# Four projections as half-size block products in a stage of their own, and a merge laid out by tokens

## The chip, the cores and the metric

The kernel runs on one core of one Trainium2 chip. The time is that of one execution on the device in microseconds (us), the median of three runs. TensorE (PE) multiplies matrices into PSUM, VectorE (DVE) and ScalarE (ACT) work on SBUF and PSUM, GpSimd (POOL) on SBUF alone; SyncE (SP), ScalarE and GpSimd have queues from which DMAs start.

## What is computed

One layer of a hybrid decoder for 512 tokens of width 1024, in float32. The parts of it that matter here:

```python
h = rms_norm(x, mixer_norm)
q, k, v, g_out, a_lr, z, xbc, dt, gate_a, gate_b = split_cols(h @ w_in)   # v, g_out, gate_a, gate_b: 1024 wide
o_a = gla_mixer(q, k, v, g_out, a_lr, ...)      # 4 heads, dk 128, dv 256, chunks of 64; o * rsqrt(mean(o*o)) * silu(g_out)
o_b = ssd_mixer(z, xbc, dt, ...)                # 2048 wide, 4 groups, chunks of 128
merged = sigmoid(gate_a) * (o_a @ w_branch_a) + sigmoid(gate_b) * (o_b @ w_branch_b)
x = x + merged @ w_out
h = rms_norm(x, ffn_norm)
act, lin = split(h @ w_ffn_up)                  # 2816 each
x = x + (gelu(conv3(act)) * lin) @ w_ffn_down
x = x + sigmoid(rms_norm(x, ple_norm) @ w_ple_gate) * (p @ w_ple_proj)
return rms_norm(x, final_norm)
```

## The kernel before

Every float32 product is made of three fast ones. An operand is split into a rounded part and the rest: `wsplit` (L160) lets ScalarE cast a raw weight tile to `whi` (L164) and VectorE subtract it to get `wlo` (L165), 1024 columns at a time. Three matmuls follow (`mm3`, L168, and the loops at L249 and L348): high by high, high by low, low by high. The normed activations lie turned, features on partitions, as `hT` (h1h and h1l, eight blocks of 128 features by 512 tokens). There are four buffers each of whi and wlo, and a ring of raw weight tiles, two up to the feed-forward part and five in it; raw tiles come by DMA from SP's queue (`wload`, L149).

`proj_a` holds weights still and moves activations, so that its result has features on partitions. `proj_b` holds activations still and moves 512 weight columns, so that its result has tokens on partitions. Both take PSUM banks from `mm_ps`, of which there are four; everything else (transposes, GLA's and SSD's small products) takes banks in turn from the other four, `sm_ps`.

The stages follow one another. SSD runs over four groups: x, B and C by `proj_a`, z by `proj_b`, the core of four chunks, the gate, and `ssd_branch` (L679), which multiplies a group's output by 512 rows of w_branch_b and adds it into `accb`, features on partitions. The last group's branch (L787) has a lower priority and so lies beside the start of GLA. GLA (L792 to L962) first makes the decay from a small gate product (`gg`, L807), then for each pair of heads the projections of v, of q and k, and of the output gate (`gla_pair_proj`, L828), and then one core per head (`gla_core`, L881). A core computes att and atc, masks them (L896), turns ks into kst, builds the state from u in four steps, makes the four outputs o, squares and sums them on ScalarE (L936), takes the root on GpSimd (`ors`, L357), gates them by `sg` on VectorE (L940) and turns them into `oah` and `oal`. Then come the merge gates (`gate_pair`, L970) by `proj_a`, with GpSimd multiplying the second gate by accb (L977), between pieces of w_branch_a (`branch_pair`, L985), which yield the merged activations turned already, `mth` and `mtl`. w_out by `proj_b`, the residual and the norm follow, then the feed-forward part.

The feed-forward down projection already uses seven half-size products in place of eight (`strassen`, L328, with `STEPS`, L279): activations are combined by `combine` (L289, VectorE), weight quarters are added by DMA (L318) or by GpSimd (L325), the products gather in three pairs of PSUM banks X, Y and Z, and after each step VectorE adds both banks into x.

A planner orders the instructions of each engine when the program is built. It simulates their times and takes what is ready by priority; `ahead` (L136) raises that of a weight's load and split and of the work that empties a bank. On the chip each engine and queue then goes through its list in order.

Of the kernel before, what the change touches and what calls it, by code (L numbers as in the profile page):

```python
# [43 lines left out]
def tile_hybrid_block(  # L44
# [128 lines left out]
    def proj_a(srcs, act, nk, emit, halves=False, raws=None):  # L173
# [26 lines left out]
        while i < len(srcs):  # L200
# [4 lines left out]
            for s in range(0, n, per):  # L205
                with ahead():
                    hi, lo = wsplit(raw[:, :, s * P : (s + per) * P], nk, per * P)
                for j in range(per):
                    ps = mm_ps(f"pa{uid()}")
                    for k in range(nk):  # L210
# [8 lines left out]
                        )  # L219
                    with ahead(50000):  # L220
                        emit(i + s + j, ps)
            i += n

    def proj_b(src, act, nk, emit, tail=False, split_last=False):
# [17 lines left out]
        for i, t in order:  # L242
# [46 lines left out]
    def combine(pool, g2, ch, cl, j):  # L289

        t = pool.tile([P, 4, 256], F32, tag="cmb", name=f"cmb{uid()}", bufs=1)
# [14 lines left out]

    def weights(r, v, parts, kh):


        n = len(parts)  # L310
        if n < 3:
            raw = r[parts] = rp[0].tile([P, kh, 512], F32, tag="raw", name=f"raw{uid()}", bufs=rp[1])
            for i, q in enumerate(parts):
                blk = v[int(q[0]) - 1][:, :, 512 * int(q[1]) - 512 : 512 * int(q[1])]
                if i == 0:
                    nc.sync.dma_start(raw, blk)
                else:
                    nc.gpsimd.dma_start(raw, blk, accum_op=ALU.add)  # L318
# [922 lines left out]
```

## Time and profile before

| | us |
|---|---|
| median of three runs | 1177.1 |
| lowest, highest | 1175.6, 1180.19 |
| the profiled execution | 1180.49 |
| its span, first to last instruction | 1178.5 |
| TensorE busy in the span | 1157.1 (98%) |
| VectorE | 677.4 (57%) |
| ScalarE | 520.5 (44%) |
| GpSimd | 171.1 (15%) |

The profile is one execution. A matmul's recorded duration overlaps those of its neighbours, so durations add up to more than the time they fill. In a group's row stand the line and engine, the operation, what it writes and reads, the count, the busy time and mean duration in nanoseconds, and the idle time ahead of it with what ended that.

### The profile page before, as it was taken

The numbers are of one execution on the slowest core, as the hardware profiler recorded it, in microseconds if no ns is written. First come the engines' busy times: TensorE is split into PE (matmuls) and PEld (weight loads), VectorE is DVE, ScalarE is ACT, GpSimd is POOL, SyncE is SP. The second block draws the span as 40 slices with busy tenths as digits, with TensorE's granted clock in tenths as the row PEclk, the third lists the DMA queues.
The fourth block names the chain that finished last, engine by engine and source line by source line (L and its number), as shares of the span: only waits on it lengthen the run. The fifth ranks groups of instructions, "written<-read, shape, count | busy, mean of one in ns | idle before, by whom it ended". The sixth has DMA issues, their size and how long they took to land.

```text
span 1178.5 us, 14049 instructions
## 1 busy us (share of the span) xinstructions
PE 1157.1 (98%) x5540; PEld 957.9 (81%) x5540; DVE 677.4 (57%) x864; ACT 520.5 (44%) x850; POOL 171.1 (15%) x175
## 2 busy tenths in 40 slices
PE   6999999999999999999999999999999999999997
PEld 6887887887887678888888888898888888888786
DVE  5767638667558537234234324565566755766764
ACT  4566373582383217442433222444434443344553
POOL 6103004022004000000011110100021000201313
PEclk9998999999999999999999999999999999999999
DMA  7332122222223134322224232752526453445221
GB/s 209 108 106 72 37 73 72 72 72 72 89 65 98 36 110 140 107 72 72 72 72 120 77 107 72 186 154 81 134 72 170 119 158 90 116 129 123 90 90 71
DMA packets 150177, 117.39 MB, mean 100 GB/s; under 512 B 5456, under 2 KB 124880, under 8 KB 150112
## 3 DMA queue, kind: packets, MB, share of 16 engines
q1 hardware_dynamic: 146624, 108.64, 31.6%
q0 software_dynamic: 2912, 5.77, 2.9%
q10 hardware_dynamic: 576, 2.10, 0.5%
q8 instruction: 43, 0.70, 0.3%
q14 instruction: 22, 0.18, 0.0%
HBM read 114.40 MB, written 2.10 MB: 99 GB/s over the span
## 4 chain that ended last, share of the span: by engine, by line
PE 96%; DVE 1%; DMA 1%; SPq 1%; POOL 1%; issue 0%; ACT 0%; POOLq 0%; ACTq 0%
PE pa L170 18%; PE pa L169 18%; PE pa L171 17%; PE pb L249 8%; PE pb L251 8%; PE pb L250 8%; PE yd L624 3%; PE sX L348 2%; PE sX L349 2%; PE sX L350 2%; PE st L632 1%; PE yo L621 1%; PE sZ L348 1%; PE sZ L349 1%; PE sZ L350 1%; DMA raw<-in_w_in_dram 1%
## 5 line engine op out<-in xcount | busy, mean ns | idle before, releaser
L165 DVE TENSOR_TENSOR wlo<-raw,whi 128x1024 fp32r<-128x1024 f32 (+1 forms) x208 | 261.5, 1263 | 255.2 <-ACT whi L164 255.0
L164 ACT CAST whi<-raw 128x1024 fp32r<-128x1024 f32 (+1 forms) x209 | 216.9, 1039 | 359.5 <-PE pa L170 219.2
L169 PE MATMUL pa<-h1h,whi 128*128 128x512 f32 (+1 forms) x416 | 160.5, 386 | 0.3 <-ACT h1h L419 0.3
L171 PE MATMUL pa<-h1h,wlo 128*128 128x512 f32 (+1 forms) x416 | 157.7, 379 | 0.0
L170 PE MATMUL pa<-h1l,whi 128*128 128x512 f32 (+1 forms) x416 | 157.0, 377 | 0.1
L169 PE MATMUL pa<-h2h,whi 128*128 128x512 f32 (+1 forms) x384 | 142.7, 372 | 0.0
L170 PE MATMUL pa<-h2l,whi 128*128 128x512 f32 (+1 forms) x384 | 142.6, 372 | 0.0
L171 PE MATMUL pa<-h2h,wlo 128*128 128x512 f32 (+1 forms) x384 | 142.3, 372 | 0.0
L249 PE MATMUL pb<-whi,h1h 128*128 128x512 f32 x256 | 99.7, 394 | 0.8 <-DVE accb L684 0.8
L250 PE MATMUL pb<-wlo,h1h 128*128 128x512 f32 x256 | 99.8, 390 | 0.0
L251 PE MATMUL pb<-whi,h1l 128*128 128x512 f32 x256 | 99.4, 392 | 0.0
L169 PEld LDWEIGHTS pa<-h1h,whi 128*128 128x128 f32 x416 | 79.9, 192 | 15.3 <-issue 1.2
L170 PEld LDWEIGHTS pa<-h1l,whi 128*128 128x128 f32 x416 | 79.6, 191 | 14.7 <-issue 1.0
L171 PEld LDWEIGHTS pa<-h1h,wlo 128*128 128x128 f32 x416 | 79.5, 191 | 13.8 <-issue 0.2
L171 PEld LDWEIGHTS pa<-h2h,wlo 128*128 128x128 f32 x384 | 72.3, 188 | 12.6
L169 PEld LDWEIGHTS pa<-h2h,whi 128*128 128x128 f32 x384 | 72.3, 188 | 12.5
L170 PEld LDWEIGHTS pa<-h2l,whi 128*128 128x128 f32 x384 | 72.3, 188 | 12.3
L249 PEld LDWEIGHTS pb<-whi,h1h 128*128 128x128 f32 x256 | 48.1, 188 | 10.6 <-DVE accb L684 1.2
L251 PEld LDWEIGHTS pb<-whi,h1l 128*128 128x128 f32 x256 | 48.1, 188 | 9.8
L250 PEld LDWEIGHTS pb<-wlo,h1h 128*128 128x128 f32 x256 | 48.1, 188 | 9.3
L549 DVE SCALAR_TENSOR_TENSOR acc<-pa,prm,acc 128x511 f32<-128x511 f32 (+2 forms) x72 | 52.6, 743 | 2.9 <-ACT acc L547 2.0
L170 PE MATMUL pa<-obl,whi 128*128 128x512 f32 x128 | 51.9, 406 | 0.0
(378 smaller groups left out, 1995.3 us busy)
## 6 DMA issues: line engine op xcount, KB each, us to landing
raw<-in_w_in_dram SPq DMA_DIRECT2D x48, 512.0 KB, 5.1
raw<-in_w_ffn_up_dram SPq DMA_DIRECT2D x44, 512.0 KB, 5.3
raw<-in_w_in_dram SPq DMA_DIRECT2D x16, 1024.0 KB, 5.1
raw<-in_w_ffn_down_dram SPq DMA_DIRECT2D x10, 1024.0 KB, 5.2
raw<-in_w_branch_b_dram SPq DMA_DIRECT2D x32, 256.0 KB, 4.1
raw<-in_w_branch_a_dram SPq DMA_DIRECT2D x8, 512.0 KB, 4.7
raw<-in_w_out_dram SPq DMA_DIRECT2D x4, 1024.0 KB, 5.1
raw<-in_w_ffn_down_dram POOLq DMA_DIRECT2D x4, 1024.0 KB, 8.6
```

The costliest lines, as they stand in the source:

```text
L164: S.copy(hi, raw)
L165: eng.tensor_tensor(lo, raw, f32(hi), op=ALU.subtract)
L169: TE.matmul(ps, lhsT=lh, rhs=rh, start=first, stop=False)
L170: TE.matmul(ps, lhsT=lh, rhs=rl, start=False, stop=False)
L171: TE.matmul(ps, lhsT=ll, rhs=rh, start=False, stop=last)
L249: TE.matmul(pss[t], lhsT=a, rhs=hi[:, kk, :], start=first, stop=False)
L250: TE.matmul(pss[t], lhsT=a, rhs=lo[:, kk, :], start=False, stop=False)
L251: TE.matmul(pss[t], lhsT=b, rhs=hi[:, kk, :], start=False, stop=last)
L348: TE.matmul(ps, lhsT=a_h, rhs=hi[:, k % 2, :], start=new and k == 0, stop=False, skip_group_check=True)
L349: TE.matmul(ps, lhsT=a_h, rhs=lo[:, k % 2, :], start=False, stop=False, skip_group_check=True)
L350: TE.matmul(ps, lhsT=a_l, rhs=hi[:, k % 2, :], start=False, stop=k == kh - 1, skip_group_check=True)
L549: V.scalar_tensor_tensor(out=acc[:, s:], in0=ps[:, : T - s], scalar=cw[:, ct, 3 - s : 4 - s], in1=acc[:, s:], op0=ALU.mult, op1=ALU.add,)
```

## The change

Four 1024-wide projections of h1 (v, the output gate, both merge gates) leave GLA and the merge and become a stage between SSD and GLA. Each is one `strassen` product of seven steps, in the order `ORDER`, with four raw quarters loaded once and summed on GpSimd in place (`weights_once`); its pieces are gathered in SBUF, put through their function and stored to DRAM from ScalarE's queue, 256 KB each. Blocks of h1 are used as they are; four further combinations of them are made once (`hc`), the sums by GpSimd. GLA's pairs and the merge load the pieces back from SP's queue. The ring has five raw tiles in the new stage, and two in GLA. w_branch_b, w_branch_a and accb are laid out by tokens (`proj_b`), so that the merged result is turned by TensorE (`transpose_split`) before w_out. In GLA ks, qi and the third exponential are made in place, kst and on have two buffers, sg six. The residual x2 reuses accb's buffers, and `ssd_gate` is parted from the turning of its result (`ssd_turn`). The core of the diff:

```diff
-    def combine(pool, g2, ch, cl, j):
...
+    ORDER = (0, 4, 1, 3, 2, 5, 6)
+    def combine(pool, g2, at, j, cs=(0, 3, 2, 5), eng=V):
         a1, a21, a22 = g2[:, :, :256], g2[:, 0, 256:], g2[:, 1, 256:]
-        V.tensor_tensor(t[:, 0, :], a22, a21, op=ALU.subtract)
-        V.tensor_tensor(t[:, 3, :], t[:, 0, :], a1[:, 0, :], op=ALU.add)
-        V.tensor_tensor(t[:, 1, :], a1[:, 0, :], a21, op=ALU.subtract)
-        V.tensor_tensor(t[:, 2, :], t[:, 3, :], a1[:, 1, :], op=ALU.subtract)
-        for c, src in ((slice(0, 2), a1), (2, a22), (3, t[:, 0, :]), (slice(5, 7), t[:, 1:3, :])):
-            S.copy(ch[:, c, j, :], src)
-            V.tensor_tensor(cl[:, c, j, :], src, f32(ch[:, c, j, :]), op=ALU.subtract)
-        S.activation(ch[:, 4, j, :], t[:, 3, :], AF.Copy, scale=-1.0)
-        V.scalar_tensor_tensor(
-            out=cl[:, 4, j, :], in0=t[:, 3, :], scalar=-1.0, in1=f32(ch[:, 4, j, :]),
-            op0=ALU.mult, op1=ALU.subtract,
-        )
+        def tmp():
+            return pool.tile([P, 2, 256], F32, tag="cmb", name=f"cmb{uid()}", bufs=2)
+        def put(c, n, src):
+            h, l, c = at(c)
+            c = slice(c, c + 2) if n == 2 else c
+            S.copy(h[:, c, j, :], src)
+            V.tensor_tensor(l[:, c, j, :], src, f32(h[:, c, j, :]), op=ALU.subtract)
+        if 0 in cs:
+            put(0, 2, a1)
+        if 3 in cs:
+            t = tmp()
+            eng.tensor_tensor(t[:, 0, :], a22, a21, op=ALU.subtract)
+            eng.tensor_tensor(t[:, 1, :], t[:, 0, :], a1[:, 0, :], op=ALU.add)
+            put(3, 1, t[:, 0, :])
+            h, l, c = at(4)
+            S.activation(h[:, c, j, :], t[:, 1, :], AF.Copy, scale=-1.0)
+            V.scalar_tensor_tensor(
+                out=l[:, c, j, :], in0=t[:, 1, :], scalar=-1.0, in1=f32(h[:, c, j, :]),
+                op0=ALU.mult, op1=ALU.subtract,
+            )
+        if 2 in cs:
+            put(2, 1, a22)
+        if 5 in cs:
+            t = tmp()
+            eng.tensor_tensor(t[:, 0, :], a1[:, 0, :], a21, op=ALU.subtract)
+            eng.tensor_tensor(t[:, 1, :], a22, a1[:, 1, :], op=ALU.subtract)
+            eng.tensor_tensor(t[:, 1, :], t[:, 1, :], t[:, 0, :], op=ALU.add)
+            put(5, 2, t)
...
-    def strassen(src, ch, cl, kh, add):
+    def weights_once(r, v, n, kh):
+        if not r:
+            for q in ("11", "12", "21", "22"):
+                r[q] = new_raw(kh)
+                nc.sync.dma_start(r[q], quarter(v, q))
+        dst, src = {0: ("11", 0), 4: ("21", 0), 1: ("11", "12"), 3: ("22", 0), 2: ("11", "22"), 5: ("12", "22"), 6: ("11", "21")}[n]
+        if src:
+            pool_sum(r[dst], r[src], kh)
+        return r[dst]
+    def strassen(src, get, kh, add, once=True, ybank=None):
         v = src.rearrange("(k two p) n -> two p k n", two=2, p=P)
         banks, r = {}, {}
-        for n, (c, parts, b, th, h, sign) in enumerate(STEPS):
+        for n in ORDER if once else range(7):
+            c, parts, b, th, h, sign = STEPS[n]
             with ahead():
-                raw = r[parts] if parts in r else weights(r, v, parts, kh)
+                raw = weights_once(r, v, n, kh) if once else weights(r, v, parts, kh)
                 ws = [wsplit(raw[:, k : min(k + 2, kh), :], min(2, kh - k), 512) for k in range(0, kh, 2)]
             new = b not in banks
             if new:
-                banks[b] = [sm_ps(f"s{b}{uid()}") for _ in range(2)]
+                banks[b] = [(ybank or sm_ps if b == "Y" else sm_ps)(f"s{b}{uid()}") for _ in range(2)]
...
+                    a_h, a_l = get(c, k, tok)
...
+    def project_out(off, fn, dst):
+        cnt, pcs = Parts(), {}
+        def add(t, h, ps, sign, n):
+            first, last = cnt(t, h)
+            if first:
+                pcs[t, h] = hsp.tile([P, T], F32, tag="pj", name=f"pj{uid()}", bufs=8)
+            pc = pcs[t, h]
+            if first and last:
+                S.activation(pc, ps, fn)
+            elif first:
+                S.activation(pc, ps, AF.Copy, scale=float(sign))
+            else:
+                V.tensor_tensor(pc, pc, ps, op=ALU.add if sign > 0 else ALU.subtract)
+                S.activation(pc, pc, fn)
+            if last:
+                nc.scalar.dma_start(dst[t][h], pc)
+        return strassen(w_in[:, off : off + 1024], hget, 4, add, ybank=mm_ps)
...
     def ssd_branch(g):
-        def emit(n, ps):
+        def emit(t, h, ps):
             if g == 0:
-                S.copy(accb[:, n, :], ps)
+                accb[t][h] = piece_of(f"accb{t}_{h}")
+                S.copy(accb[t][h], ps)
             else:
-                V.tensor_tensor(accb[:, n, :], accb[:, n, :], ps, op=ALU.add)
-        proj_a(
-            [w_branch_b[512 * g : 512 * (g + 1), n * P : (n + 1) * P] for n in range(KD)],
-            st[g]["ob"], 4, emit,
-        )
+                V.tensor_tensor(accb[t][h], accb[t][h], ps, op=ALU.add)
+        for h in range(2):
+            yield from proj_b_steps(
+                w_branch_b[512 * g : 512 * (g + 1), 512 * h : 512 * h + 512], st[g]["ob"], 4,
+                lambda t, ps, h=h: emit(t, h, ps), tail=True,
+            )
...
-    base = tc.cur_priority
-    tc.cur_priority = base + 1200
-    ssd_branch(SG - 1)
-    tc.cur_priority = base
+    run(ssd_branch(SG - 1))
     sx.close()
+    ex_ = ExitStack()
+    hsp = ex_.enter_context(tc.tile_pool(name="hsp", bufs=1, reuse_waits="tile"))
+    ring(ex_, 5)
+    hc = [hsp.tile([P, 4, 4, 256], R, name=f"hc{c}") for c in "hl"]
+    def h_at(c):
+        return hc[0], hc[1], c - 3
+    def hget(c, k, tok):
+        if c > 2:
+            return combs(h_at)(c, k, tok)
+        f = 2 * k + (c > 0)
+        tok = slice(tok.start + 256 * (c == 2), tok.stop + 256 * (c == 2))
+        return hT[0][:, f, tok], hT[1][:, f, tok]
+    dv = project_out(OFF_V, AF.Copy, vd)
+    run(dv, 2)
+    for j in range(4):
+        pr = hsp.tile([P, 2, T], F32, tag="pair", name=f"hpair{j}", bufs=1)
+        G.tensor_tensor(pr, f32(hT[0][:, 2 * j : 2 * j + 2, :]), f32(hT[1][:, 2 * j : 2 * j + 2, :]), op=ALU.add)
+        combine(hsp, pr, h_at, j, (3, 5), G)
+    run(dv)
+    run(project_out(OFF_G, AF.Silu, sgd))
+    run(project_out(OFF_GA, AF.Sigmoid, gad))
+    run(project_out(OFF_GB, AF.Sigmoid, gbd))
+    ex_.close()
...
-            E3 = gp.tile([P, T], F32, tag="E3", name=f"E3_{h}", bufs=2)
+            E3 = bc
...
-        v = v0 if hp2 == 0 else gp.tile([P, NT, 512], F32, tag="v", name=f"v{hp2}", bufs=2)
-        sg = gp.tile([P, NT, 512], F32, tag="sg", name=f"sg{hp2}", bufs=1)
-        proj_b(
-            w_in[:, OFF_V + 512 * hp2 : OFF_V + 512 * (hp2 + 1)], hT, KD,
-            lambda t, ps: S.copy(v[:, t, :], ps),
-        )
+        v = gp.tile([P, NT, T], F32, tag="v", name=f"v{hp2}", bufs=2)
+        sg = [gp.tile([P, T], F32, tag="sg", name=f"sg{hp2}_{t}", bufs=6) for t in range(NT)]
+        for t in range(NT):
+            nc.sync.dma_start(v[:, t, :], vd[t][hp2])
+        for t in range(NT):
+            nc.sync.dma_start(sg[t], sgd[t][hp2])
...
-        proj_b(
-            w_in[:, OFF_G + 512 * hp2 : OFF_G + 512 * (hp2 + 1)], hT, KD,
-            lambda t, ps: S.activation(sg[:, t, :], ps, AF.Silu),
         )
...
-        qi = gp.tile([P, T], F32, tag="qi", name=f"qi{h}", bufs=1)
-        S.copy(ev(qi, 0), ev(qtl, 0))
+        ks, qi = kpr, qtl
+        V.tensor_tensor(ev(ks, 0), ev(kpr, 0), dv[:, :, 1:2].to_broadcast([P, 4, 64]), op=ALU.mult)
         V.tensor_tensor(ev(qi, 1), ev(qtl, 1), dv[:, :, 0:1].to_broadcast([P, 4, 64]), op=ALU.mult)
-        ks = gp.tile([P, T], F32, tag="ks", name=f"ks{h}", bufs=1)
-        S.copy(ev(ks, 1), ev(kpr, 1))
-        V.tensor_tensor(ev(ks, 0), ev(kpr, 0), dv[:, :, 1:2].to_broadcast([P, 4, 64]), op=ALU.mult)
...
+    rp[:] = mring
+    gtp = gx.enter_context(tc.tile_pool(name="gtp", bufs=1, reuse_waits="tile"))
+    def gate(d, t, h):
+        gt = gtp.tile([P, T], F32, tag="gt", name=f"gt{uid()}", bufs=8)
+        nc.sync.dma_start(gt, d[t][h])
+        return gt
+    gas = [[gate(gad, t, h) for t in range(NT)] for h in range(1)]
+    for h in range(2):
+        for t in range(NT):
+            G.tensor_tensor(accb[t][h], accb[t][h], gate(gbd, t, h), op=ALU.mult)
     mtp = gx.enter_context(tc.tile_pool(name="mtp", bufs=1, reuse_waits="tile"))
...
-    gate_pair(0)
-    gate_pair(2)
-    branch_pair(0)
...
+    mt = tuple(mtp.tile([P, KD, T], R, name=f"mt{c}") for c in "hl")
+    def branch_a(h):
+        ga = gas[0] if h == 0 else [gate(gad, t, 1) for t in range(NT)]
+        def emit(t, ps):
+            ac = accb[t][h]
+            V.tensor_tensor(ga[t], ga[t], ps, op=ALU.mult)
+            V.tensor_tensor(ac, ac, ga[t], op=ALU.add)
+            transpose_split(ac, mt, t, h, f"mT{t}")
+        proj_b(w_branch_a[:, 512 * h : 512 * h + 512], (oah, oal), KD, emit, tail=h == 1)
+    for h in range(2):
+        branch_a(h)
+    x2 = [[piece_of(f"x2_{t}_{h}") for h in range(2)] for t in range(NT)]
+    for h in range(2):
+        for t in range(NT):
+            nc.sync.dma_start(x2[t][h], x[t * P : (t + 1) * P, 512 * h : 512 * h + 512])
...
```

## Rows read from the trace of the kernel before

**Rows 1.** The page: busy time by engine; the chain that ended last.

```profile
PE 1157.1 (98%) x5540; PEld 957.9 (81%) x5540; DVE 677.4 (57%) x864; ACT 520.5 (44%) x850; POOL 171.1 (15%) x175
...
PE 96%; DVE 1%; DMA 1%; SPq 1%; POOL 1%; issue 0%; ACT 0%; POOLq 0%; ACTq 0%
```

**Rows 2.** Waits, TensorE: waiter, awaited, us in all, times, longest.

```profile
PE xn0T L417 <- DVE xn L394: 7.4, 1, 7.4
...
PE pb L249 <- DVE accb L684: 0.8, 1, 0.8
...
PE sX L349 <- DVE wlo L165: 0.6, 1, 0.6
...
PE ot L670 <- DVE Xg L664: 0.2, 1, 0.2
```

**Rows 3.** Windows by stage: length, then busy (count) by engine, clock, DMA.

```profile
396.00:484.00 88.00, 87.22 (x371) 68.62 (x370) 43.77 (x60) 33.19 (x43) 0.00 (x0) 1.00 0.36 115
484.00:546.00 62.00, 62.00 (x300) 51.18 (x299) 25.10 (x40) 29.00 (x55) 3.73 (x8) 1.00 0.26 75
```

**Rows 4.** Timeline of TensorE, 121 to 128 us: start, duration.

```profile
121.24 0.40 PE L170 MATMUL pa<-h1l,whi 128*128 128x512 f32 x1
...
127.82 0.39 PE L169 MATMUL pa<-h1h,whi 128*128 128x512 f32 x1
```

**Rows 5.** Chain in order of time: start, length, what, matmul instructions.

```profile
509.98 0.43 PE o L921 x2
...
510.84 0.44 PE oaT L947 x4
511.28 0.89 PE att L890 x8
...
754.81 0.87 PE x2n0T L417 x8
```

**Rows 6.** Groups by line and form: GpSimd, VectorE, ScalarE.

```profile
L325 POOL TENSOR_TENSOR raw<-raw,raw 128x1024 f32<-128x1024 f32 x10 | 24.7, 2469 | 106.7 <-DVE wlo L165 106.7
...
L977 POOL TENSOR_TENSOR sgt<-sgt,accb 128x512 f32<-128x512 f32 x8 | 14.1, 1768 | 76.6 <-ACT sgt L975 76.6
...
L896 DVE TENSOR_TENSOR attT<-att,gmask 128x512 f32<-128x512 f32 x4 | 2.8, 692 | 1.8 <-PE att L890 1.8
...
L911 ACT COPY kstok<-kst 128x512 f32<-128x512 f32 x4 | 2.3, 579 | 1.6 <-PE kst L909 1.6
```

**Rows 7.** Timelines of VectorE, then of GpSimd, 870 to 890 us.

```profile
877.32 0.69 DVE L1087 TENSOR_TENSOR x<-x,sX 128x512 f32<-128x512 f32 x1
...
879.82 1.23 DVE L165 TENSOR_TENSOR wlo<-raw,whi 128x1024 fp32r<-128x1024 f32 x1
...
881.55 3.04 DVE L165 TENSOR_TENSOR wlo<-raw,whi 128x1024 fp32r<-128x1024 f32 x1
...
876.96 2.52 POOL L325 TENSOR_TENSOR raw<-raw,raw 128x1024 f32<-128x1024 f32 x1 [3.05 <-DVE wlo L165]
881.12 2.40 POOL L325 TENSOR_TENSOR raw<-raw,raw 128x1024 f32<-128x1024 f32 x1 [1.65 <-DVE wlo L165]
```

**Rows 8.** DMA issues: size of one, us from issue to landing.

```profile
raw<-in_w_in_dram SPq DMA_DIRECT2D x16, 1024.0 KB, 5.1
```

**Rows 9.** Timeline of the first GLA core, 509.5 to 519.5 us.

```profile
510.25 0.59 PE L923 MATMUL o<-gS,qi 128*128 128x256 f32 x2
...
511.16 0.19 ACT L936 ACTIVATION_READ_ACCUMULATOR on<-o 128x1 f32 x1
...
511.44 0.19 POOL L356 TENSOR_SCALAR ors<-oss 128x2 f32<-128x2 f32 x1 [5.56 <-ACT on L936]
...
512.82 0.87 DVE L940 SCALAR_TENSOR_TENSOR on<-o,ors,sg 128x256 f32<-128x256 f32 x2
```

**Rows 10.** Timeline of TensorE at 109 us, and a later window.

```profile
109.25 2.12 PE L624 MATMUL yd<-xdt,L 128*128 128x64 f32 x16 [1.58 <-DVE xdt L617]
...
118.00:120.00 2.00, 2.00 (x8) 1.48 (x8) 0.66 (x2) 0.76 (x3) 0.00 (x0) 0.50 0.05 12
```

More of the change, by code (lines that the diff above doesn't have):

```diff
@@ new lines, in combs, with get, quarter, new_raw @@
+    def combs(at):
+        def get(c, k, tok):
+            h, l, c = at(c)
+            return h[:, c, k, tok], l[:, c, k, tok]
+        return get
+    def quarter(v, q):
+        return v[int(q[0]) - 1][:, :, 512 * int(q[1]) - 512 : 512 * int(q[1])]
+    def new_raw(kh):
+        return rp[0].tile([P, kh, 512], F32, tag="raw", name=f"raw{uid()}", bufs=rp[1])
+    def pool_sum(dst, src, kh):
+        for k in range(0, kh, 2):
+            q = slice(k, min(k + 2, kh))
+            G.tensor_tensor(dst[:, q, :], dst[:, q, :], src[:, q, :], op=ALU.add)
@@ L317, in weights @@
                 else:
-                    nc.gpsimd.dma_start(raw, blk, accum_op=ALU.add)
+                    nc.gpsimd.dma_start(raw, quarter(v, q), accum_op=ALU.add)
             return raw
         raw, more = (r["11", "12"], "22") if n == 3 else (r["11", "12"], "21")
-        if (more,) not in r:
-            weights(r, v, (more,), kh)
-        for k in range(0, kh, 2):
-            q = slice(k, min(k + 2, kh))
-            G.tensor_tensor(raw[:, q, :], raw[:, q, :], r[more,][:, q, :], op=ALU.add)
@@ L326, in weights @@
-        return raw
-    def strassen(src, ch, cl, kh, add):
+        pool_sum(raw, weights(r, v, (more,), kh), kh)
+        return raw
+    def weights_once(r, v, n, kh):
[7 more added lines that the diff above has]
+        return r[dst]
@@ L353, in strassen, with __init__, __call__, ready @@
             yield
+    class Parts:
+        def __init__(self):
+            self.left = {}
+        def __call__(self, t, h):
+            total = 1 if (t // 2, h) == (1, 0) else 2
+            n = self.left.get((t, h), total)
+            self.left[t, h] = n - 1
+            return n == total, n == 1
+    class TileNorms:
+        def __init__(self, pool, tag, bufs, x, gain, dst, name):
+            self.a = pool, tag, bufs, x, gain, dst, name
+            self.nm = {}
+        def ready(self, t, h):
+            pool, tag, bufs, x, gain, dst, name = self.a
+            first = t not in self.nm
+            if first:
+                self.nm[t] = Norm(pool, x[t], f"{name}{t}", tag, bufs)
+            self.nm[t].square(h)
+            if first:
+                self.nm[t].gather()
+            else:
+                norm_T(self.nm[t], gain, dst, t)
+    def run(d, n=1000):
+        for _ in range(n):
+            if next(d, d) is d:
+                return
     def rsqrt_mean(dst, ssq, inv, n):
@@ L781, in tile_hybrid_block @@
         ssd_gate(g)
+        ssd_turn(g)
         if g + 1 < SG:
@@ L815, in tile_hybrid_block @@
         gtmp.append(e)
+    dx.close()
+    oap = gx.enter_context(tc.tile_pool(name="oap", bufs=1, side="right", reuse_waits="tile"))
+    oah = oap.tile([P, KD, T], R, name="oah")
+    oal = oap.tile([P, KD, T], R, name="oal")
+    glaring = rp[:]
+    ring(gx, 2, "right")
+    mring = rp[:]
+    rp[:] = glaring
     for h in range(GH):
@@ L985, in branch_pair @@
-    def branch_pair(n0):
-        def emit(i, ps):
-            n = n0 + i
-            s = gates[0, n]
-            V.tensor_tensor(s, s, ps, op=ALU.mult)
-            V.tensor_tensor(s, s, gates[1, n], op=ALU.add)
-            S.copy(mth[:, n, :], s)
-            V.tensor_tensor(mtl[:, n, :], s, f32(mth[:, n, :]), op=ALU.subtract)
-        proj_a([w_branch_a[:, (n0 + i) * P : (n0 + i + 1) * P] for i in range(2)], (oah, oal), KD, emit)
-    gate_pair(0)
-    gate_pair(2)
-    branch_pair(0)
-    gate_pair(4)
```

191 lines of the change are left out of this document (84 added, 107 removed).

## The prediction

> **What bounds the kernel now.** I read the page first: TensorE is busy for 98% of the span, VectorE for 57%, ScalarE for 44%, GpSimd for 15%, and the chain that ended last is TensorE for 96% [rows 1]. A busy TensorE may still be waiting inside a pipelined matmul, so the second view was what TensorE waited for: under 14 us in all, 9 of them in the start, and in the part that is changed a single wait of 0.8 us (ten rows, 13.7 us together) [rows 2]. The third was the windows by stage: from 396 to 546 us, which hold branch_b's last group, GLA's first projections and its first two cores, TensorE is busy 87.2 of 88 us and then 62 of 62, at full granted clock [rows 3]. So until about 775 us time is what TensorE issues. Removed matmuls count at their issue spacing, not at the mean that the groups print: in a stretch without gaps 29 matmuls of 512 columns start between 121.24 and 127.82 us, 0.2269 us each [rows 4].
>
> **The change part by part.** The sum is made against the profiled execution, 1180.5 us (span 1178.5). The median of the three runs, 1177.1, lies 3.4 lower, and I take that off at the end.
>
> *Matmuls removed.* The projections of values, output gates and the two merge gates are each 512x1024 times 1024x1024: 8 k blocks, 8 output tiles, 3 products, so 192 matmuls. As seven half-size products each takes 7 x 2 x 4 x 3 = 168. Four of them save 96, at 0.2269 us 21.8 us.
>
> *Transposes added.* Merge by tokens needs its result turned: 4 token tiles x 2 halves x 4 = 32 transposes. Eight take 0.87 us [rows 5], so 32 take 3.5. branch_b and branch_a keep their matmul counts (96 per group, 192) when the operands swap sides, and branch_b's adds into accb stay 512 wide. The ends are the same: +3.5.
>
> *Half-size products: who must keep up.* A step is 24 matmuls, 5.44 us, a projection 38.1. ScalarE has 14 casts, six copies and eight functions, which at 1.23 us each (a wlo of the same width as a cast, the widest of them) would be 34.4, so it keeps up. VectorE has 14 wlo subtractions, 1.23 us when alone [rows 7], and 6 adds from PSUM at 0.69: 17.2 + 4.1. GpSimd has four block sums of two 2.47 us pieces [rows 6]: 19.8. These are not independent. At 881.55 us a wlo that began while GpSimd summed took 3.04 us against 1.23, and it ended at 884.59, as one of some 1.1 us would that began when the sum ended at 883.52; an add from PSUM at 877.32, inside a sum that ran from 876.96, took 0.69 [rows 7]. So sums and wlo exclude each other: 17.2 + 19.8 = 37.0 of 38.1 us if the PSUM adds go beside the sums, and 41.1 if none do. That is a cost of 0 to 3.0 us a projection, 0 to 12 in all. [...] I take 2: adds arrive two to a step, there is room for them beside sums, and the first projection starts with a lead, as below. The combinations of the activations (GpSimd: four pairs of one 1024-wide and five 256-wide operations, 4 x (2.47 + 5 x 0.62) = 22.3 us, a quarter of the 1024-wide one taken for the narrow) are first needed at the third step. They read h1 alone, so the planner can put them under the last branch_b (96 matmuls, 21.8 us) and the first two steps (10.9): 32.7 us for 22.3 of work. Nothing is added; without that cover it would be 22.3.
>
> *DMA.* Weight blocks come as 1 MB, 5.1 us from issue to landing [rows 8], 20 of 38.1 us for four. The one late block reuses the buffer that the last sum of the projection before frees: some 2.4 us of splits, 5.3 to land, 4.9 of sums and 2.4 of splits make 15.0 us, from that buffer's last split, which can be done a step and a quarter before its products start, to the third step of the next projection, 17 us ahead at least. Hidden, by 2 us. The 32 stores of 256 KB sit on ScalarE's queue behind the function that made the piece, and the values are read a hundred us later. Behind them on ScalarE stand the next casts, a step ahead of need. The loads stand on SP's queue among weight loads; v and sg have the 21.8 us of the q and k projection to arrive.
>
> *From the last product to GLA.* The q and k weights go to memory that the combinations hold until the sixth of the seven steps ends. Then 5.1 us to land, and a cast and a wlo at 1.23 each: 7.6 us, against a last step of 5.44. Ends 0 (GLA's four small gate matmuls, whose weights have long been loaded, fill the rest) and 7.6; I take 2, the difference.
>
> *GLA's cores lose cover.* Before, the second pair's values, q, k and gates (65 us of matmuls) stood beside the first two cores and 87 us of merge gates beside the last two. Afterwards q and k alone (96 matmuls, 21.8 us) stand beside the first, and beside the last only branch_a's first half for heads 0 to 2: 72 matmuls, 16.3 us, 5.4 of it only when head 2 is done. The chain of one core, from rows: att and atc at most 0.89 each, mask 0.69 and ks 0.35 (half as wide; it is now in place, so after atc), kst 0.44 (four transposes, as oaT's four), its copy 0.58, u 0.43 (as o), its copy 0.29 (half as wide), then from the issue of the second o to the end of the gating 3.44 (510.25 to 513.69), u again 0.43 (its bank is one that the gating frees), the state 0.44 (as one gating), o to gating once more 3.44, oaT 2 x 0.44 [rows 5, 6, 9]: 13.2, and with 0.1 us at eight further hand-overs (an estimate from 511.35, where a sum was read out, to 511.44, where ors began) 14.0. The next core's att reuses a bank that the last gating frees, so a pair takes 28.0, of which 14.8 is TensorE's own (1.78 + 0.44 + ten of 0.43 + 0.88 a core). 13.2 us are waiting per pair. The first pair has 21.8 of cover. The second has 10.9 that is free from the start: 2.3 short, then some 1.4 for head 3's oah and oal (two as wide as the mask) before the last quarter of branch_a, and about 1 because ors stands on GpSimd behind accb's gating of 1.77 us an operation [rows 6]. Ends 0 and 13.2; I take 5.
>
> *At nothing:* the 0.8 us wait that goes with accb, the two copies per core that go, one more narrow operation per combine in the feed-forward part (its TensorE is full), x2 into accb's buffers (loaded 20 us ahead of use).
>
> Sum: -21.8 + 3.5 + 2 + 2 + 5 = -9.3. 1180.5 becomes 1171.2, and on the scale of the median **1168**.
>
> **The rivals.**
>
> *A, as summed:* 1168, give or take 5.
>
> *B, everything hidden.* -18.3: 1159. For it speaks the planner, which leaves no wait over 1.6 us after the start [rows 2, 10]; against it the cover that is used up beside the last two cores.
>
> *C, sums and wlo.* At the dear end the four projections take 12 us more than TensorE needs, not 2: 1168 + 10 = 1178, no change that can be measured (under 0.5%, 5.9 us). For it, the exclusion of [rows 7]; against it, that the down products of the feed-forward part show two such sums in a row and TensorE waits 0.6 us there in all [rows 2], though they have fewer sums per product (two of the seven blocks, where the change sums four).
>
> [...]
>
> That the change doesn't remove what it says can be left out: counts are in the code.
>
> **How the numbers follow.** A 0.45, B 0.18, C 0.22, D 0.15. Faster by over 0.5% is under 1171.2: A's part below it 0.37, B 0.18, a corner of C 0.04: 0.59. Same: A's upper edge 0.08 and C's middle 0.15: 0.23. Slower is above 1183: D and C's upper edge, 0.18. The range goes from B with a little to spare, 1156, to between C and D, 1185, leaving out most of D; the likeliest case's own is 1163 to 1173.
>
> **What would show it.** TensorE should issue 64 fewer instructions (96 less, 32 more). The stage of products should last 152.4 us with TensorE waiting for wlo for under 4; over 10 there is C. [...] It is wrong altogether if the part before 390 us or after the first feed-forward projection changes length by more than some us, since neither is argued here.

## Result, and the profile after

The changed kernel takes 1207.4 us (median of 4 runs, 1205.8 to 1211.4) against 1176.4 for the kernel before, run beside it: a ratio of 1.0245, 95% interval 1.0213 to 1.0277. It is 2.5% slower where 0.8% faster was forecast, and outside the range. Its profiled span is 1205.4 us, 26.9 longer.

The page of the changed kernel, as in [rows 1]: busy time by engine, and the chain that ended last.

```profile
PE 1152.9 (96%) x5476; PEld 947.7 (79%) x5476; DVE 780.1 (65%) x935; ACT 558.4 (46%) x899; POOL 293.4 (24%) x231
...
PE 85%; DVE 5%; POOL 3%; ACT 2%; issue 2%; DMA 1%; SPq 1%; ACTq 0%; POOLq 0%; DVEq 0%
```

TensorE issues the 64 instructions less that were counted, but it is busy only 4.2 us less, and idle 52.5 us of its span instead of 21.4. Where the idle time lies is seen in the windows of the changed kernel (length, then busy time and count by engine, granted clock, DMA share, GB/s), as in [rows 3]:

```profile
0.00:385.00 385.00, 371.65 (x1907) 307.71 (x1907) 255.11 (x306) 203.38 (x371) 86.98 (x88) 1.00 0.28 85
385.00:450.00 65.00, 55.22 (x230) 42.69 (x229) 54.43 (x47) 24.31 (x36) 53.98 (x33) 0.92 0.30 105
450.00:585.00 135.00, 133.46 (x579) 107.76 (x578) 98.93 (x71) 75.97 (x96) 75.31 (x27) 1.00 0.43 148
585.00:650.00 65.00, 57.27 (x247) 45.28 (x246) 33.97 (x49) 30.47 (x45) 0.91 (x2) 0.92 0.47 147
650.00:750.00 100.00, 92.92 (x445) 73.91 (x444) 50.90 (x83) 32.69 (x66) 17.03 (x22) 0.97 0.39 137
750.00:800.00 50.00, 45.07 (x236) 38.88 (x235) 23.01 (x30) 15.63 (x30) 4.05 (x12) 0.93 0.39 103
```

The kernel before is idle 11.8 us in the first of these stretches, 1.5 in the second and 0 in the others up to 800 us. So the 31 us are: 1.5 in the first, 8.3 about the first projection of the new stage, 1.5 in the rest of the stage, 7.7 at the step to GLA, 7.1 about the cores and 4.9 at the start of the feed-forward part.

The clock takes more. In the changed kernel TensorE's granted clock was 0.50 in six stretches between 394 and 795 us, each in or behind a hole in its work; in the kernel before in one, at 111 us [rows 10]. These are the windows at 0.50, the six as their sum, then the one before:

```profile
sum 34.00, PE 23.60 PEld 18.75 DVE 26.04 ACT 15.21 POOL 13.60; mean PE 3.93 PEld 3.13 DVE 4.34 ACT 2.54 POOL 2.27
110.90:121.20 10.30, 9.62 (x26) 5.97 (x26) 8.39 (x13) 5.18 (x8) 4.69 (x5) 0.50 0.37 104
```

In these stretches matmuls of 512 columns start 0.427 us apart (599.54 to 602.53 us in the changed kernel, at 0.50), against 0.227 from 603.22 us on, at 1.00. Here and below I count half of the busy time at 0.50 as lost, an estimate a little above what these two spacings give, 0.47: 11.8 of 23.6 us, against 4.8 of 9.6 before, 7.0 more. By the counts busy time should fall by 18.3 us, and it fell by 4.2. So 7.1 us are left that neither the counts nor the clock explain; they were not taken apart. Part of them may be that the last matmul ahead of a stop counts with its full 0.39 us, and not with the 0.23 to the next one.

What ended the idle time, TensorE's waits in the changed kernel, as in [rows 2] (waiter, awaited, us in all, times, longest):

```profile
PE pa L180 <- DVE wlo L174: 7.8, 2, 7.3
...
PE sX L418 <- ACT whi L173: 7.2, 2, 6.5
PE x2n3T L523 <- DVE x2n L500: 2.8, 1, 2.8
PE atc L1061 <- DVE attT L1066: 2.2, 2, 1.4
PE pa L178 <- ACT whi L173: 2.1, 3, 1.6
PE ot L813 <- DVE Xg L804: 2.0, 2, 1.7
```

Before, the longest wait in the changed part was 0.8 us. Now six pairs behind the start have 2 us or more in all.

**The first projection.** GpSimd's timeline in the changed kernel, in its third step and ahead of it (start, length):

```profile
390.03 2.36 POOL L954 TENSOR_TENSOR hpair<-h1h,h1l 128x1024 f32<-128x1024 f32 x1
...
422.93 2.85 POOL L366 TENSOR_TENSOR raw<-raw,raw 128x1024 f32<-128x1024 f32 x1
...
427.42 1.77 POOL L343 TENSOR_TENSOR cmb<-hpair 128x256 f32<-128x256 f32 x1
...
437.72 3.33 POOL L366 TENSOR_TENSOR raw<-raw,raw 128x1024 f32<-128x1024 f32 x1
441.01 1.71 POOL L330 TENSOR_TENSOR cmb<-hpair 128x256 f32<-128x256 f32 x1
```

Sums (`raw`) and combinations (`hpair`, `cmb`) alternate in one queue, and each is longer than priced: a 256-wide addition up to 1.77 us (priced 0.62), a sum up to 3.4 (2.47). The third step breaks off: TensorE stands still from 435 to 441.65 us, starts two matmuls of the fifth step, and goes on with the third at 443.21, with the combination whose `cmb` began at 441.01, behind the sum of 437.72. The two matmuls had waited for a cast on ScalarE that stood behind a piece of the step before; VectorE's addition to that piece stood behind a `wlo` of 2.78 us. From 443 to 446 the granted clock is 0.50; from 446 it is 1.00 again. The groups by line of the changed kernel (busy time, mean ns of one):

```profile
L174 DVE TENSOR_TENSOR wlo<-raw,whi 128x1024 fp32r<-128x1024 f32 x224 | 319.9, 1441 | 204.8 <-ACT whi L173 204.5
L366 POOL TENSOR_TENSOR raw<-raw,raw 128x1024 f32<-128x1024 f32 x42 | 119.9, 2866 | 163.3 <-DVE wlo L174 163.3
```

**The step to GLA.** VectorE and TensorE after the last product in the changed kernel (in brackets, idle time before and what ended it):

```profile
594.46 0.75 DVE L977 TENSOR_SCALAR ge<-gg,prm 128x512 f32<-128x512 f32 x1 [4.78 <-DMA v<-vd]
...
597.67 1.22 DVE L174 TENSOR_TENSOR wlo<-raw,whi 128x1024 fp32r<-128x1024 f32 x1
...
598.95 0.80 PE L180 MATMUL pa<-h1h,wlo 128*128 128x512 f32 x1 [7.29 <-DVE wlo L174]
```

The last gate tile `ge` lies in memory where a piece of the last product waits for its store; `wlo`, which TensorE needs, stands behind it on VectorE. The view names a load as the releaser, but `ge` waits for the semaphore that the store sent off at 588.50 raises (a load that waits for the same one left at 594.35), while the DMA engines were full (share 1.00, 327 GB/s, at 590 to 598 us).

**The feed-forward start.** SP's waits from 735 to 800 us in the changed kernel:

```profile
SPq L163 <- PE pb L271: 35.8, 1, 35.8
```

The second weight load lies over the merged activations, so it and all behind it in SP's queue wait for the output projection's last matmul. From the transposes of the third token tile to the end it is 424.4 us, 415.9 before: 8.5 lost after the part that the prediction argued. All of it lies at the start: from the 193rd matmul of the feed-forward part to the end it is 391.3 us, 391.2 before.

### The profile page after: what moved, and what is told of

It reads as the page before. It is cut to its first block, busy times and chain, and to the rows that moved or that the text cites. A ratio compares the mean times of both kernels' runs of the same rounds, so it can differ in the third digit from the quotient of the medians.

```text
span 1205.4 us, 14211 instructions
## 1 busy us (share of the span) xinstructions
PE 1152.9 (96%) x5476; PEld 947.7 (79%) x5476; DVE 780.1 (65%) x935; ACT 558.4 (46%) x899; POOL 293.4 (24%) x231
## 4 chain that ended last, share of the span: by engine, by line
PE 85%; DVE 5%; POOL 3%; ACT 2%; issue 2%; DMA 1%; SPq 1%; ACTq 0%; POOLq 0%; DVEq 0%
PE pa L180 11%; PE pa L178 11%; PE pa L179 11%; PE pb L269 8%; PE pb L270 8%; PE pb L271 8%; PE sX L418 4%; PE sX L419 3%; PE sX L420 3%; PE yd L763 2%; DVE wlo L174 2%; PE sZ L418 2%; PE sZ L419 2%; PE sZ L420 1%; POOL raw L366 1%
## 5 line engine op out<-in xcount | busy, mean ns | idle before, releaser
L174 DVE TENSOR_TENSOR wlo<-raw,whi 128x1024 fp32r<-128x1024 f32 (+1 forms) x232 | 325.9, 1419 | 210.8 <-ACT whi L173 210.5
L173 ACT CAST whi<-raw 128x1024 fp32r<-128x1024 f32 (+1 forms) x233 | 240.7, 1040 | 265.3 <-PE pa L179 141.7
L366 POOL TENSOR_TENSOR raw<-raw,raw 128x1024 f32<-128x1024 f32 (+1 forms) x44 | 123.4, 2817 | 167.3 <-DVE wlo L174 167.3
L180 PE MATMUL pa<-h1h,wlo 128*128 128x512 f32 (+1 forms) x288 | 108.3, 376 | 7.3 <-DVE wlo L174 7.3
L178 PE MATMUL pa<-h1h,whi 128*128 128x512 f32 (+1 forms) x288 | 109.3, 379 | 0.7 <-ACT whi L173 0.4
L179 PE MATMUL pa<-h1l,whi 128*128 128x512 f32 (+1 forms) x288 | 108.6, 377 | 0.1
L180 PEld LDWEIGHTS pa<-h2h,wlo 128*128 128x128 f32 x384 | 73.4, 191 | 13.2 <-DVE wlo L174 0.8
L178 PEld LDWEIGHTS pa<-h1h,whi 128*128 128x128 f32 x288 | 56.2, 195 | 11.6 <-ACT whi L173 1.7
L270 PE MATMUL pb<-wlo,obh 128*128 128x512 f32 x128 | 53.0, 414 | 0.0
L269 PE MATMUL pb<-whi,obh 128*128 128x512 f32 x128 | 52.4, 410 | 0.1
L271 PE MATMUL pb<-whi,obl 128*128 128x512 f32 x128 | 50.2, 396 | 0.0
L269 PE MATMUL pb<-whi,h1h 128*128 128x512 f32 x128 | 50.1, 394 | 0.0
```

Of the source, the lines that this page charges most:

```text
L173: S.copy(hi, raw)
L174: eng.tensor_tensor(lo, raw, f32(hi), op=ALU.subtract)
L178: TE.matmul(ps, lhsT=lh, rhs=rh, start=first, stop=False)
L179: TE.matmul(ps, lhsT=lh, rhs=rl, start=False, stop=False)
L180: TE.matmul(ps, lhsT=ll, rhs=rh, start=False, stop=last)
L269: TE.matmul(pss[t], lhsT=a, rhs=hi[:, kk, :], start=first, stop=False)
```

## Experiments

Each kernel is the changed one with the edit shown. Times are compared by the ratio to the kernel before that ran beside them.

| run | us | ratio to before | 95% interval | span |
|---|---|---|---|---|
| changed | 1207.4 | 1.0245 | 1.0213 to 1.0277 | 1205.4 |
| e1_vsum | 1197.7 | 1.0171 | 1.0126 to 1.0216 | 1202.9 |
| e2_vcomb | 1196.8 | 1.0164 | 1.0125 to 1.0203 | 1200.8 |
| e3_ringfirst | 1203.1 | 1.0208 | 1.0170 to 1.0246 | 1198.9 |
| e4_ffnring | 1207.8 | 1.0241 | 1.0204 to 1.0277 | 1205.0 |
| e5_gates | 1204.1 | 1.0225 | 1.0201 to 1.0249 | 1202.3 |
| e6_ffnearly | 1197.5 | 1.0181 | 1.0158 to 1.0205 | 1195.9 |
| e7_vboth | 1189.6 | 1.0115 | 1.0085 to 1.0145 | 1193.4 |
| e8_all | 1184.8 | 1.0062 | 1.0038 to 1.0086 | 1183.3 |
| e9_qkearly | 1173.1 | 0.9942 | 0.9920 to 0.9963 | 1171.7 |
| e10_gpsimd | 1184.4 | 1.0052 | 1.0029 to 1.0076 | 1182.6 |
| e11_gatev | 1172.9 | 0.9951 | 0.9928 to 0.9974 | 1171.4 |

**e1_vsum, e2_vcomb, e7_vboth: which engine adds.**

```diff
# e1
-            pool_sum(r[dst], r[src], kh)
+            pool_sum(r[dst], r[src], kh, V)
# e2
-        G.tensor_tensor(pr, f32(hT[0]...
+        V.tensor_tensor(pr, f32(hT[0]...
-        combine(hsp, pr, h_at, j, (3, 5), G)
+        combine(hsp, pr, h_at, j, (3, 5), V)
# e7: both
```

> The changed kernel with one edit: the block sums of the new stage's weights (12 of its 28 products, two adds of 1024 columns each) are made by VectorE instead of GpSimd; the combinations of the activations stay on GpSimd. Theory 1: GpSimd's sums and VectorE's low parts hold each other up (a sum 2.8 us on average instead of 2.5, a low part up to 3.7 instead of 1.23), and this starves the products. Then the sums cost VectorE about 1.2 us each with no exclusion, TensorE's idle time between 396 and 588 us falls by 8 to 12 us, and the kernel takes about 1197 (1193 to 1201). Rival: only the first projection is starved, by the combinations in GpSimd's queue, and the sums are harmless elsewhere. Then only what GpSimd's queue gains in the first projection shows, 2 to 4 us: 1203 to 1206.

> The changed kernel with one edit: the four additions of hidden high and low parts and the 20 sums of the combinations are made by VectorE instead of GpSimd; the block sums of the weights stay on GpSimd. Theory 1: the combinations cost what they cost because they stand on GpSimd, with the sums of the first projection behind them in its queue, and because they block VectorE's work of SSD's tail at 390 us. Then the hole of 5.8 us at 436 to 443 us goes, and the kernel takes about 1200 (1197 to 1203). Rival: VectorE has no room for them either, and the hole only moves to the low parts behind them: 1205 to 1209.

> The changed kernel with both the block sums of the weights and the combinations on VectorE (e1 and e2 together). Theory 1: what e1 and e2 gave (about 8.5 and 9 us by their ratios) came from different places, e1 from the three projections after the first, e2 from the first and the SSD tail, and adds up in part: about 1193 (1190 to 1197). Rival: VectorE is full in the first projection (35 to 39 of 39 us in e1 and e2), so both together starve TensorE there, and the kernel is no faster than either alone: 1196 to 1202.

`wlo` from 450 to 585 us in the changed kernel, then `wlo` and the sums there in e1:

```profile
L174 DVE TENSOR_TENSOR wlo<-raw,whi 128x1024 fp32r<-128x1024 f32 x47 | 84.9, 1839 | 26.2 <-ACT whi L173 26.0
...
L174 DVE TENSOR_TENSOR wlo<-raw,whi 128x1024 fp32r<-128x1024 f32 x47 | 57.3, 1222 | 25.4 <-ACT whi L173 24.8
L366 DVE TENSOR_TENSOR raw<-raw,raw 128x1024 f32<-128x1024 f32 x26 | 30.6, 1220 | 0.2
```

On VectorE a sum takes 1.22 us, and `wlo` is back at 1222 ns on average. From 450 to 585 us TensorE is then idle 0 us (1.5 in the changed kernel), so what engines can still win in the stage lies ahead of that: from 385 to 450 it is busy 55.2 us in the changed kernel, 57.8 in e1, 60.0 in e2, 62.2 in e7, out of 65. The gains of e1 and e2 there, 2.6 and 4.7, add up to about what e7 has, 7.0. By the ratios the gains are larger, 0.7%, 0.8% and 1.3%, some 9, 10 and 15 us. e1's profiled span is only 2.5 us shorter, but its profile has TensorE busy 13.0 us at a clock of 0.50 at 112 to 126 us, ahead of all that the edit touches, where the changed kernel's has none: 6.5 us lost, counted as above, that hide most of its gain. Theory 1 of e1 asked for 8 to 12 us less idle time by 588 us; it was 4.1. e7 shows that VectorE, busy 39 of 39 us at 397 to 436, does not become the bound by it: TensorE is busy for 38.6 of these 39.

**e3_ringfirst, e5_gates: the tiles at the step to GLA.**

```diff
# e3: the weight buffers of the stage first
+    ring(ex_, 5)
     hsp = ex_.enter_context(tc.tile_pool(name="hsp", ...))
-    ring(ex_, 5)
# e5: pieces in a pool of their own behind the combinations;
# GLA's gsm, ge, E1, E2 and on in a pool egp, which lies over hsp alone
+    pjp = ex_.enter_context(tc.tile_pool(name="pjp", ...))
-            pcs[t, h] = hsp.tile(
+            pcs[t, h] = pjp.tile(
+    egp = ggx.enter_context(tc.tile_pool(name="egp", ...))
```

> The changed kernel with one edit: the five weight buffers of the new stage are opened before its other tiles, so that the first gate tiles of GLA lie over a weight buffer and no longer over the pieces whose stores are the last to leave. Theory 1: the 7.3 us in which TensorE waits at 590 to 600 us for a low part come from the gate tile's wait for a store, with the low part queued behind it on VectorE. Then the stretch 585 to 600 us is nearly full, and the kernel takes about 1199 (1196 to 1202). Rival: the weights of Q and K are late anyway, since the DMA engines are full (328 GB/s) at 580 to 600 us; then the wait only changes its name: 1204 to 1208.

> The changed kernel with the pieces in a pool of their own behind the combinations, and GLA's gate and exponential tiles in a pool that lies over the combinations alone. Opening the weight buffers first (run e3) gave the 585 to 600 us stretch back, and then lost 8.8 us at the first attention product, because the gate chain still began at 589 us: its tiles lay over a pool that the list order could hand out only when all work on it had been placed. Theory 1: the tiles' place sets when the gate chain starts. It now starts about 15 us earlier, ahead of the low parts of Q and K, both waits go, and the kernel takes about 1193 (1189 to 1198), 13 less than the changed kernel by its ratio. Rival: GLA's start has too much serial work between the last product and the first attention product whatever the layout; then at most what e3 gave comes back: 1199 to 1204.

In e3 TensorE is busy all of 585 to 600 us (7.3 of 15 in the changed kernel), so the tiles' place over the stored pieces was the cause; but then its longest wait is a new one:

```profile
PE att L1060 <- DVE E L1022: 8.8, 1, 8.8
```

In e5 the gate chain starts at 582 us, 5 ahead of the last product's end (in e3 at 589, 2 behind it), both of these waits are gone, and the next one steps up:

```profile
PE pa L178 <- ACT whi L173: 7.5, 3, 4.2
```

5.8 us of this, in two waits, are for the high part of Q's first weights, whose buffer lies over the combinations until the last product that reads them. e3 gains 0.4% and e5 0.2%; their intervals overlap the changed kernel's. Theory 1 of e5 failed; the time is the one that its rival gave, but not by the rival's cause, as e9 shows below: with other places for the tiles the stretch from 585 to 600 us is full but for 0.7 us. Three waits stood one behind the other, and one edit alone only brought up the next.

**e4_ffnring, e6_ffnearly: the feed-forward start.**

```diff
# e4: the norm's tiles and 16 KB of nothing between the gates and mt
+    xnp = gx.enter_context(tc.tile_pool(name="xnp", ...))
+    pad = gx.enter_context(tc.tile_pool(name="pad", bufs=1)).tile([P, 4096], F32, ...)
     mtp = gx.enter_context(tc.tile_pool(name="mtp", ...))
# e6: the first two weight blocks in free memory, issued ahead of w_out's loop
+    f0p = gx.enter_context(tc.tile_pool(name="f0p", ...))
+    for o in (0, FH):
+        f0.append(f0p.tile([P, KD, 2 * P], F32, name=f"f0_{o}"))
+        for i in range(2):
+            nc.sync.dma_start(f0[-1][:, :, i * P : (i + 1) * P], ...)
```

> The changed kernel with one edit: the tiles of the gates, of the merged activations and of the norm are laid out so that the first three weight buffers of the feed-forward part lie over tiles that are free long before the output projection ends (an unused stretch of 16 KB keeps the merged activations off them). Theory 1: the feed-forward start loses about 8.5 us because its second weight load waits on SP's queue for the output projection's last matmul (35.8 us of waiting), and everything behind it in that queue too. Then the first feed-forward matmul comes 4 to 5 us earlier after the last transposes of the normed activations, the clock returns sooner, and the kernel takes about 1199 (1197 to 1202). Rival: the chain of the norm alone holds the start, and the weights would only wait for it: 1205 to 1208.

> The changed kernel with the first two weight blocks of the feed-forward part in two tiles of their own, over memory that nothing uses then. Run e4 had these weights loaded early as well and gained nothing, because ScalarE's order had their high parts behind the last casts of the normed activations. Theory 1: the pool that they lie over decides their place in the order, and with a place of their own the casts stand ahead of the last norms, as in the kernel before; TensorE's first feed-forward matmul then follows within a microsecond of the second or third transposes, the stretch 780 to 800 us is nearly full, and the kernel takes about 7 less than the changed kernel: 1200 (1197 to 1203). Rival: the norm's chain of the last token tile holds the start anyway: 1205 to 1208.

e4 gained nothing. Its loads left from 743.43 us, but in its ScalarE timeline the casts of the weights stand behind the last cast of the norm, with no idle time between:

```profile
785.93 0.58 ACT L525 CAST h2h<-x2n3T 128x512 fp32r<-128x512 f32 x1 [0.27 <-PE x2n3T L523]
786.41 3.89 ACT L173 CAST whi<-raw 128x1024 fp32r<-128x1024 f32 x4
```

So not the data but the order was late: each engine's order is fixed ahead of the run, and these casts came after everything in the pools that their buffers overlap. In e6, with a place of their own, TensorE's timeline shows the first feed-forward matmul ahead of the third token tile's transposes, as in the kernel before:

```profile
779.76 0.28 PE L178 MATMUL pa<-h2h,whi 128*128 128x256 f32 x1
...
779.88 1.04 PE L523 MATMUL x2n2T<-ident,x2n 128*128 128x128 f32 x8
```

The stretch 750 to 800 us is full, at clock 1.00, and e6 gains 0.6%, as expected. That a pool and not a tile decides the place in the order is read from the orders of these programs and borne out by e3, e5, e6 and e9; it was not tested by itself.

**e8_all, e9_qkearly: everything together.**

```diff
# e8 = e7 + e5 + e6;  e9 = e8 and:
+    cbp = ex_.enter_context(tc.tile_pool(name="cbp", ...))   # 16 KB, where GLA's two weight buffers will lie
-        pr = hsp.tile(..., name=f"hpair{j}", bufs=1)
+        pr = cbp.tile(..., name=f"hpair{j}", bufs=2)
-        combine(hsp, pr, h_at, j, (3, 5), V)
+        combine(cbp, pr, h_at, j, (3, 5), V, 4)                     # four cmb tiles in place of two
-            ... name=f"pj{uid()}", bufs=8)
+            ... name=f"pj{uid()}", bufs=6)
```

> All repairs together: sums and combinations on VectorE, GLA's gate tiles over the combinations, the first feed-forward weights in tiles of their own. If the change's own saving of some 18 us of products less transposes is real and only the three losses hid it, the kernel comes out below the kernel before: 1172 (1164 to 1180), ratio about 0.993. If the saving itself is not there (the products run slower than the rows of the old projections say), it stays above: 1182 to 1190.

> Run e8 with one more repair: the tiles of the combinations get a pool of 16 KB at the place where GLA's two weight buffers will lie (the pieces have 6 buffers instead of 8 to make room), so that the weights of Q and K are loaded during the products and no longer wait, at 569 us, for the last product that reads the combinations. In e8 TensorE still waited 5.85 us between 570 and 600 us, 4.2 of it for the high part of Q's first weights, and its clock was 0.81 and 0.85 there. Theory 1: the step from the last product to GLA costs what the place of its first tiles costs; the hole closes, the clock stays up, and the kernel takes about 7 less than e8: 1177 (1173 to 1181), as long as the kernel before. Rival: ScalarE's chain of gate exponentials and table loads (12 us of it between 573 and 592) holds Q's high parts back wherever the weights lie: 1182 to 1186.

e8 landed where its second sentence said, but not for that cause: its products run without a gap from 450 to 570 us, and 5.8 us of waits for Q's high part are left. e9 takes those away, and is faster than the kernel before by 0.6% (0.4 to 0.8). Against e8 it gains 1.2%, 11.6 us by the spans, where its theory asked for 7: 5.1 us less idle time from 570 to 600, 3.4 us of clock there, and 1.7 us from 385 to 450, which the deeper buffers of the combinations may have given; the rest was not taken apart. Its page, then its windows:

```profile
PE 1139.4 (97%) x5476; PEld 941.4 (80%) x5476; DVE 779.5 (67%) x991; ACT 561.9 (48%) x902; POOL 169.4 (14%) x175
```

```profile
385.00:450.00 65.00, 63.14 (x289) 51.35 (x288) 60.01 (x88) 30.30 (x44) 1.20 (x2) 1.00 0.49 163
450.00:585.00 135.00, 135.00 (x586) 109.30 (x585) 103.12 (x106) 84.69 (x104) 0.64 (x2) 1.00 0.46 152
585.00:650.00 65.00, 61.28 (x306) 49.85 (x305) 37.29 (x63) 30.95 (x55) 3.56 (x8) 1.00 0.32 105
650.00:750.00 100.00, 95.72 (x445) 77.29 (x444) 48.79 (x67) 27.42 (x55) 17.94 (x22) 0.98 0.45 148
750.00:800.00 50.00, 50.00 (x325) 45.72 (x324) 32.42 (x45) 24.94 (x37) 3.86 (x6) 1.00 0.55 148
```

The same 5476 instructions now keep TensorE busy 17.7 us less than before. What is left over is 10.9 us more idle time than before, 8.0 of it in the stretches from 585 to 750 us, which hold the cores.

**e10_gpsimd: the engine again, in the mended layout.**

```diff
# e9 with
-            pool_sum(r[dst], r[src], kh, V)
+            pool_sum(r[dst], r[src], kh)
-        V.tensor_tensor(pr, f32(hT[0]...
+        G.tensor_tensor(pr, f32(hT[0]...
-        combine(cbp, pr, h_at, j, (3, 5), V, 4)
+        combine(cbp, pr, h_at, j, (3, 5), G, 4)
```

> Run e9 with the block sums and the combinations back on GpSimd, where the change had put them; all tiles stay where e9 has them. Theory 1: the places of the tiles and the engine of the sums are separate losses. From the changed kernel, moving both jobs to VectorE gave 1.3% (e7); here it is taken away again, so the kernel takes about 15 more than e9, 1188 (1184 to 1193), slower than before. Rival: on GpSimd the sums only hurt because other work stood behind them in a bad layout; with the layout mended they are covered: 1172 to 1179.

1.1% slower than e9, and slower than the kernel before: theory 1, at the low side (11 us by the spans, 13 by the ratios). Its `wlo` takes 1879 ns on average from 450 to 585 us (1222 in e9), and TensorE is idle 3.4 us there and 5.0 from 385 to 450 (0 and 1.9 in e9).

```profile
L174 DVE TENSOR_TENSOR wlo<-raw,whi 128x1024 fp32r<-128x1024 f32 x48 | 88.9, 1879 | 27.7 <-ACT whi L173 27.7
```

**e11_gatev: GpSimd's gating by the branch gate.**

```diff
# e9 with
-            G.tensor_tensor(accb[t][h], accb[t][h], gate(gbd, t, h), op=ALU.mult)
+            V.tensor_tensor(accb[t][h], accb[t][h], gate(gbd, t, h), op=ALU.mult)
```

> Run e9 with the eight multiplications of the second branch by its gate on VectorE instead of GpSimd. Theory 1: the stretch from 650 to 700 us, in which TensorE is still idle for 4.3 us, is bounded by GLA's own chains (masked attention, squares and scales of each head), not by these multiplications, so nothing is gained: 1170 to 1176. Rival: GpSimd's four at 695 us (5.5 us together) hold VectorE's gating of the other branch up, and 2 to 4 us come back: 1168 to 1170.

0.9951 against 0.9942: no difference, theory 1.

## Why the prediction was wrong

**The saving was right.** -21.8 + 3.5 = -18.3 us of matmuls; e9, with most of the holes closed, shows -17.7. What failed is that the work beside the matmuls was priced too low or at nothing, that one wait was not looked at, and that holes also cost clock. (For the late weight block the sum has 5.3 us to land where [rows 8] has 5.1; nothing hangs on it.)

**"Nothing is added" for the combinations** is the first step that failed. Cover was counted in engine time, 22.3 us under 32.7. But GpSimd's queue holds the first projection's sums too, and both engines hold each other up (a `wlo` of 2.78 us at 436.06, 1.23 when alone [rows 7]; a sum of 3.33 at 437.72, 2.47 before [rows 6]), so that the third step broke off for 6.5 us; and at 390 us the combinations also stretched four `Xg` multiplications, which end SSD's chain, from 1.91 us in the kernel before to 5.19. With the sums this made 8.3 us idle about the first projection and 3.6 of clock. The combinations alone, moved to VectorE, give back 4.7 us of the idle time and 0.8% of the time (e2).

**Sums and `wlo`**, priced 2 with ends 0 and 12: too small as well. The mechanism was right: `wlo` at 1.84 us in place of 1.23. The three later projections lose 1.5 us by it, but the first had no lead, since the combinations stood in the same queue: the sums alone, moved to VectorE, give back 0.7%, some 9 us (e1). Both together are worth 11 to 13 us (e9 against e10), so that rival C's mechanism was there. Its sign, over 10 us of waits for `wlo` in the stage, did not show: under 1 us for `wlo`, 7.2 for `whi`. That 11 to 13 lie at C's dear end of 12 is chance, since C left the combinations out. On VectorE a sum takes 1.22 us (e1), where it took 2.47 on GpSimd before [rows 6], and a `wlo` of the same width took 1.23 on VectorE even then [rows 7]: by these times the sums belonged on VectorE.

**From the last product to GLA**, priced 2 of 0 to 7.6: 7.7 idle and 2.0 of clock. The step traced the weights of Q and K alone. It missed the gate chain, whose tiles lay over pieces still to be stored, and what stands behind a waiting `ge` on VectorE. Under that wait lay a second and a third (e3, e5, e9).

**GLA's cores**, priced 5 of 0 to 13.2: 7.1 idle and 3.2 of clock, within the ends; in e9 8.0 idle and 1.6 of clock from 585 to 750 us. The term was too small by 2 us, or 5 with the clock. The longest waits there are for the mask `attT` (2.2 us in two) and for the gated output `on` (1.3 in two from 650 to 700 us); which hand-over was priced too low was not taken apart and stays open.

**The feed-forward start** was not argued; x2 in accb's buffers was put at nothing, and the merged activations were not looked at. Moving the merge to tokens moved its tiles over the next part's weight buffers: 8.5 us, of which e6 gives back 0.6%. The prediction's sign of being altogether wrong, another length after the first feed-forward projection, did not show (391.3 us against 391.2).

**The clock.** D, which the chances and the upper end of the range count with, is a lowered granted clock in the second pair of cores. No run shows the loss that it stands for there (by the chances, a time above 1183 us); in its place the changed kernel showed 0.50 from 667.9 to 671.3 us, and again from 702.0 to 705.4, where branch_a goes on; together TensorE is busy for 6.5 us in them, 3.2 of them lost. The other holes had no clock in the forecast: 0.50 at 443 to 446 us and at 598 to 602, back at 1.00 from 446 and from 603. In all the changed kernel lost 7.0 us more to the clock than the kernel before.

The sum made again from the profile: -18.3 by the counts, +7.0 by the clock, +7.1 of busy time that stays open, +31.1 of idle time, 26.9. The 7.1 are what is left over, so the sum closes by its making. In e9 the four terms are -18.3, -1.5, +2.1 and +10.9: 6.8 us less. That this comes near the 9.3 of the forecast is in part luck: it took the repair of waits that the forecast did not have, and what remains is waiting of another size, 8.0 us in the stretches that hold the cores.

## What to carry to other kernels

When a new stage is put between two others, look up which tiles of the neighbours lie at the addresses of its own, and follow each tile's last reader or store to whatever stands behind the waiter in its queue; here that was worth as much as the arithmetic saved (e7 to e9: 1.7%, 20 us, of which some 2 may be e9's deeper buffers). "Hidden under" needs the queue, not only the engine's free time: list what else the engine must do in that stretch and in which order. When one repair gives little, look which wait has taken its place before giving the theory up: e3 and e5 gave 0.4% and 0.2%, neither clear of noise, and e9 on top of e8 1.2%.

## What the runs showed of the hardware

A VectorE instruction with one tensor as input was held up as well: four `Xg` multiplications beside GpSimd's additions took 5.19 us in the changed kernel, 1.91 before and 1.68 in e9, without them:

```profile
390.09 5.19 DVE L804 TENSOR_SCALAR Xg<-Xg,yrs 128x512 f32<-128x512 f32 x4 [1.09 <-POOL yrs L463]
...
392.25 1.91 DVE L664 TENSOR_SCALAR Xg<-Xg,yrs 128x512 f32<-128x512 f32 x4 [1.35 <-POOL yrs L357]
...
391.75 1.68 DVE L804 TENSOR_SCALAR Xg<-Xg,yrs 128x512 f32<-128x512 f32 x4 [1.09 <-POOL yrs L463]
```

The first of the four took 2.58 us, until 392.67; GpSimd's addition `hpair`, begun 0.06 us ahead of it, ended at 392.39. The median of this line's 16 in the changed kernel is 0.48 us. That the two hold each other up is read from these times; by what means, no run shows. GpSimd's instructions took longer as well: its 1024-wide sum took 2.47 us on average before and 2.87 in the changed kernel, and its 256-wide additions there ranged from 0.72 to 1.77.
